# Split weights kept in DRAM by the first band of a hybrid streaming encoder; weights in pieces of four row tiles

## The chip, the cores and the metric

The kernel runs on one core of one Trainium2 chip. The metric is the device time of one execution in microseconds (us). Every time below is from that chip.

## What is computed

One layer of a hybrid encoder, on 2048 frames of a new stream and 32 frames of a running one (2080 columns in all, width 1024). Cut to what matters:

```
hn  = rmsnorm(x, norm1);   proj = hn @ w_in            # 1024 x 3072
ya  = RG-LRU group, yb = RWKV-7 group, yc = mLSTM group   # of proj, causal
x   = x + concat(ya, yb, yc) @ w_out                   # 1024 x 1024
gu  = rmsnorm(x, norm2) @ w_ffn_in                     # 1024 x 5632
x   = x + (silu(gu[..., :2816]) * gu[..., 2816:]) @ w_ffn_out   # 2816 x 1024
out = rmsnorm(x, norm_f), and the mixers' new states
```

All of it is float32.

## The kernel before, in words

Activations lie with the features on the 128 partitions and frames along the columns. The frames are cut into four **bands**: 512, 512, 512 and 544 (two blocks of 272). For each band there is an input normalisation (`innorm`), an input projection (`inproj`, 24 output tiles of 128 features), the three mixers on groups of 128 frames (`mixers`, `group`), and a second half (`phase2`: the output projection of 8 tiles, 44 tiles of the first FFN matrix in six groups, and after each group the 8 output tiles of the second FFN matrix over the 4 or 3 row tiles of that group). The program records `inproj` of all four bands first, then by turns `mixers(i)` and `phase2` of band i.

**Products.** Every big product is made with float32r operands in two parts. A value x is written as hi (its float32r copy, by ScalarE) plus lo (x - hi, by VectorE): `split`, line 618. `mm3` (623) then issues three matmuls for each row tile of 128 and each block of columns: hi x hi, hi x lo, lo x hi, summed in PSUM. The weights are read from DRAM again in every band, and split again.

**Weights.** `load_w` (590) fetches one weight tile of kt row tiles (8, or 4 and 3 for the second FFN matrix). It takes a slot for the parts, a pair `wh`, `wl` of 128 x 1024 of which there are WB = 2 (a tile of 4 or fewer row tiles takes half of one), loads the raw float32 data into one of RB = 2 buffers `raw` of 128 x 1024, and splits it. In the input projection every second tile goes, in two halves of four row tiles, into the tiles `hh0` to `hh3` and `hl0` to `hl3`, which `phase2` uses for the split FFN activations. The last group of the last band puts four of its weight tiles into activation tiles that are no longer needed (`into`).

**Order of the work.** Nothing is issued as it is written. A `Recorder` (148) takes down every instruction with a level, and `order` (244) plans them on five queues (TensorE, VectorE, ScalarE, GpSimd, and SP, which issues nearly all DMAs). Each takes, of what is ready in the plan, the lowest level first. The levels are a pair, the second for TensorE: `EVAC` (-2), `WGT` (-1; loads and splits of weights), `NORM` (0), `MIX` (1; the mixers), `PROJ` (0, and 2 on TensorE) and `LATE` (2). So on TensorE the mixers' matmuls go before those of the projections, in bursts that `order` holds back by a debt (RATE, BURST, GATHER, WAIT). Durations come from `cost` (348). A DMA costs its bytes at 360 per ns, one after the other:

```python
            if best == "dma":
                free[best] = when + 475.0
                dma_end = max(dma_end, free[best] + 650.0) + o.dur
                o.end = dma_end
                free[best] = max(free[best], dma_end - WINDOW)
```

The resulting order of each queue is fixed. On the chip each engine works through it and waits for semaphores where something is late. So an instruction that waits holds up all that stands behind it on its queue. All instructions have line 332 (`emit`) in the profile; they are told apart by the names of their tiles: `pj` is the PSUM tile of the projections, `rw` and `ml` those of the mixers, `ah`/`al` and `hh`/`hl` split activations.

**The mixers' round trip.** In `rwkv`, for each group of 128 frames, a small matrix goes from `Hr` to DRAM (`tb<-Hr`, four DMAs), comes back repeated on 96 partitions (`xs<-tb`, one DMA of 384 KB, here called the broadcast), is worked on by 62 short VectorE instructions in a row (`utmp`, `Z`), goes to DRAM once more (`zb<-Z`) and back (`c<-zb`). There are 17 groups.

Of the kernel before, what the change touches and what calls it, by code (L numbers as in the profile page):

```python
# [11 lines left out]
F32 = mybir.dt.float32  # L12
F32R = mybir.dt.float32r
# [12 lines left out]
NFF = 22  # L26
# [95 lines left out]
PSLACK = 300.0  # L122
XB = 8
ACCB = 2
WB = 2
RB = 2
HG = 4
SQB = 3
# [293 lines left out]
def hybrid_kernel(ctx, tc, A, O, cfg):  # L422
# [161 lines left out]
                return y[:, a:b, col - c0:col - c0 + n]  # L584


    half = [None]
    wide = [0]

    def load_w(src, kt, eng=None, many=False, into=None):  # L590


        if many:
            wide[0] += 1
        if into is not None:
            parts = [tuple(t[:, :kt * 128] for t in into)]
        elif many and wide[0] % 2:
            f = wide[0] // 2 % 2 * 2
            parts = [tuple(hp.tile([128, HW], F32R, tag=f"{x}{f + h}", name="w" + x)[:, :512] for x in ("hh", "hl"))
                     for h in range(2)]  # L600
        elif kt <= 4 and half[0] is not None:
            parts = [tuple(t[:, 512:512 + kt * 128] for t in half[0])]
            half[0] = None
        else:
            slot = tuple(wp.tile([128, 1024], F32R, tag=x, name=x) for x in ("wh", "wl"))
            half[0] = slot if kt <= 4 else None
            parts = [tuple(t[:, :kt * 128] for t in slot)]
        level, rec.level = rec.level, WGT
        raw = wp.tile([128, 1024], F32, tag="raw", name="raw", bufs=RB)[:, :kt * 128]
        kp = kt // len(parts)  # L610
        for h, (wh, wl) in enumerate(parts):
            r = raw[:, h * kp * 128:(h + 1) * kp * 128]
            SY.dma_start(r.rearrange("p (k m) -> p k m", k=kp), src[:, h * kp:(h + 1) * kp, :])
            split(wh, wl, r, eng)
        rec.level = level
        return [tuple(t[:, k * 128:k * 128 + 128] for t in pt) for pt in parts for k in range(kp)]

    def split(hi, lo, x, eng=None):

        S.activation(hi, x, AF.Copy)  # L620
        (eng or V).tensor_tensor(out=lo, in0=x, in1=hi.bitcast(F32), op=ALU.subtract)
# [72 lines left out]
    def innorm(i):  # L694
# [20 lines left out]
        if i == 0:  # L715
            level, rec.level = rec.level, WGT
            load(0)
            SY.dma_start(vec, A["vecs"])
            for m, ks in enumerate(((1, 2), (3, 4), (5, 6, 7))):
                first_w.append(load_w(w_in(m), 8, V, True))  # L720
                for k in ks:
                    load(k)
            rec.level = level
            setup()
            for k in range(8):
                act.append(act_tiles(k, n))
                split_x(*act[k], x[k], VV("norm1", k))
                if k > 1:
                    square(k - 2)
            square(6)  # L730
            square(7)
        else:
            for k in range(8):
                level, rec.level = rec.level, LATE
                load(k)
                rec.level = level
                square(k)
# [7 lines left out]
    def inproj(i):  # L745
# [32 lines left out]
        for m in range(24):  # L778
            if m == NEXT and i + 1 < len(cfg.sb1):
                innorm(i + 1)  # L780
            w = first_w.pop(0) if first_w else load_w(w_in(m), 8, V, True)
            pss = proj(w, act, [x_[:2] for x_ in segs])
            for (o, N, sg), ps in zip(segs, pss):
                if late is not None:
# [591 lines left out]
    def phase2(c0, blks, HG, last=False):  # L1376
# [27 lines left out]
                V.tensor_tensor(out=acc[:, o:o + N], in0=acc[:, o:o + N], in1=sq, op=ALU.add)  # L1404

        for d in range(8):
            w = load_w(A["w_out"][d], 8)
            for (o, N), ps in zip(bl, proj(w, act, bl)):
                rec.level = EVAC
                V.tensor_tensor(out=x2[d][:, o:o + N], in0=x2[d][:, o:o + N], in1=ps, op=ALU.add)  # L1410
                rec.level = NORM
            accum(d, 0, n)
# [13 lines left out]
        for kg in groups:  # L1426
            hs = []
            for f in range(f0, f0 + kg):
                wg = load_w(A["w_ffn_in"][f], 8)
                wu = load_w(A["w_ffn_in"][NFF + f], 8)  # L1430
                hh = hp.tile([128, HW], F32R, tag=f"hh{f - f0}", name=f"hh{f - f0}")[:, :n]
                hl = hp.tile([128, HW], F32R, tag=f"hl{f - f0}", name=f"hl{f - f0}")[:, :n]
                us = []
                for (o, N), pg in zip(bl, proj(wg, act, bl)):
                    rec.level = EVAC
# [15 lines left out]
            for bs in ([[b] for b in bl] if end and last else [bl]):  # L1451
                for d in range(8):
                    if d not in ws:
                        ws[d] = load_w(A["w_ffn_out"][d][:, f0:f0 + kg, :], kg, into=act[d] if end and last and d > 3 else None)
                    for (o, N), ps in zip(bs, proj(ws[d], hs, bs)):
                        rec.level = EVAC
                        V.tensor_tensor(out=x2[d][:, o:o + N], in0=x2[d][:, o:o + N], in1=ps, op=ALU.add)
                        rec.level = NORM
                        if end:
                            accum(d, o, N)  # L1460
                            S.activation(x2[d][:, o:o + N], x2[d][:, o:o + N], AF.Copy, scale=VV("norm_f", d))
# [15 lines left out]
    mls = Pool("mls", 1)  # L1477
    dt_ = Pool("dt", 2, space=DRAM)
    ap_ = Pool("act", 1)
    wp = Pool("wp", WB)  # L1480
    ev = Pool("ev", 2)
    hp = Pool("hp", 1)
    UN = [rws.tile([128, 3, 2, 64], F32, name=f"Un{c}") for c in range(2)]
    for u in UN:
        G.memset(u, 0.0)
# [152 lines left out]
```

## Time and profile before

| | |
|---|---|
| median of 3 runs | 2850.44 us (2846.54 to 2855.05) |
| the profiled execution's own time | 2846.7 us |
| its span, first to last instruction | 2844.9 us |
| TensorE, VectorE, ScalarE busy | 2749.6, 2146.1, 1281.1 us |
| mean granted TensorE clock | 0.987 |
| DMA | 317.92 MB, mean 112 GB/s |
| HBM read, written | 268.50 MB, 46.27 MB |

All views below are of that one execution. Busy is the time in which an engine worked on at least one instruction; matmuls overlap, and the end of each is modelled, so TensorE's busy time tells above all where it was idle. The granted clock is the share of its full speed that TensorE was allowed. A wait is put down to what came last by the profile.

### The profile page before, as it was taken

Reading aid. Unit: us, or ns where it says so; the run is one execution under the profiler, and the core shown is the slowest. Engines: PE = TensorE matmul, PEld = TensorE weight load, DVE = VectorE, ACT = ScalarE, POOL = GpSimd, SP = SyncE. Lnnn points to the kernel's source line nnn. Section 1 sums busy time; section 2 is a strip of 40 time slices with the busy share of each in tenths; the row PEclk is TensorE's granted clock in tenths of the full one; section 3 lists DMA queues with packets and bytes.
Section 4 is the critical chain, followed back from the end, with each engine's and each line's share of the span. In section 5 each row is a group of like instructions: output and inputs, shape, how many; then the busy total and the mean of one; then the engine's idle time right before and its main releaser. Section 6 shows DMA issues by size and latency. Waiting matters only on the chain. (4 is left out here: it accounts for less than half of the span.)

```text
span 2844.9 us, 48298 instructions
## 1 busy us (share of the span) xinstructions
PE 2749.6 (97%) x17609; PEld 2310.6 (81%) x17609; DVE 2146.1 (75%) x6009; ACT 1281.1 (45%) x2830; POOL 43.7 (2%) x170
## 2 busy tenths in 40 slices
PE   9999999999999999999999999999999999999998
PEld 7877777889777777777777777777787778999997
DVE  6778877877887878789878888888676676554555
ACT  5555554655553444455444444454433334322223
POOL 0000000000000000000000000000000000000000
PEclk9999999999999999999999999999999999999999
DMA  7453534444323333335233333353332235232232
GB/s 238 133 168 116 179 105 143 138 132 121 121 72 108 88 100 99 95 112 160 73 108 98 89 96 94 100 162 78 100 109 83 84 89 161 81 89 87 88 93 77
DMA packets 235210, 317.92 MB, mean 112 GB/s; under 512 B 63100, under 2 KB 146988, under 8 KB 234844
## 3 DMA queue, kind: packets, MB, share of 16 engines
q1 hardware_dynamic: 233820, 313.72, 37.3%
q8 instruction: 138, 2.26, 0.3%
q10 hardware_dynamic: 1152, 1.11, 0.1%
q14 instruction: 100, 0.82, 0.1%
HBM read 268.50 MB, written 46.27 MB: 111 GB/s over the span
## 5 line engine op out<-in xcount | busy, mean ns | idle before, releaser
L332 PE MATMUL pj<-ah,wh 128*128 128x512 f32 (+1 forms) x2560 | 898.7, 359 | 3.2 <-ACT wh L332 1.1
L332 PE MATMUL pj<-al,wh 128*128 128x512 f32 (+1 forms) x2560 | 898.9, 358 | 2.5 <-DVE al L332 2.5
L332 PE MATMUL pj<-ah,wl 128*128 128x512 f32 (+1 forms) x2560 | 828.8, 356 | 1.5 <-DVE wl L332 1.5
L332 ACT ACTIVATE wh<-raw 128x1024 fp32r<-128x1024 f32 (+2 forms) x444 | 382.3, 861 | 728.8 <-PE pj L332 604.8
L332 PEld LDWEIGHTS pj<-ah,wh 128*128 128x128 f32 x2560 | 484.5, 190 | 68.7 <-ACT ah L332 1.6
L332 PEld LDWEIGHTS pj<-al,wh 128*128 128x128 f32 x2560 | 486.7, 190 | 63.9 <-DVE al L332 3.4
L332 PEld LDWEIGHTS pj<-ah,wl 128*128 128x128 f32 x2560 | 454.9, 189 | 66.8 <-DVE wl L332 3.1
L332 DVE TENSOR_TENSOR wl<-raw,wh 128x1024 fp32r<-128x1024 f32 (+2 forms) x444 | 433.0, 976 | 62.1 <-ACT wh L332 56.4
L332 PE MATMUL pj<-hh,wh 128*128 128x512 f32 (+1 forms) x856 | 299.6, 360 | 9.4 <-ACT hh L332 9.2
L332 PE MATMUL pj<-hl,wh 128*128 128x512 f32 (+1 forms) x856 | 300.9, 359 | 0.1
L332 PE MATMUL pj<-hh,wl 128*128 128x512 f32 (+1 forms) x856 | 280.9, 357 | 0.0
L332 DVE TENSOR_TENSOR x<-x,pj 128x512 f32<-128x512 f32 (+1 forms) x280 | 159.2, 584 | 126.4 <-PE pj L332 122.3
L332 PEld LDWEIGHTS pj<-hh,wh 128*128 128x128 f32 x856 | 160.9, 189 | 35.1 <-ACT hh L332 13.8
L332 PEld LDWEIGHTS pj<-hl,wh 128*128 128x128 f32 x856 | 162.3, 190 | 22.6 <-DVE hl L332 1.7
L332 PE MATMUL pj<-ah,hh 128*128 128x512 f32 (+1 forms) x480 | 170.1, 361 | 6.6 <-ACT hh L332 5.8
L332 PEld LDWEIGHTS pj<-hh,wl 128*128 128x128 f32 x856 | 152.8, 189 | 22.2
L332 PE MATMUL pj<-al,hh 128*128 128x512 f32 (+1 forms) x480 | 169.6, 360 | 0.0
L332 PE MATMUL pj<-ah,hl 128*128 128x512 f32 (+1 forms) x480 | 156.9, 359 | 0.0
L332 DVE TENSOR_TENSOR utmp<-Z,xs 96x60 f32<-96x60 f32 (+27 forms) x527 | 107.0, 203 | 59.1 <-DMA xs<-tb 52.5
L332 DVE TENSOR_TENSOR stg<-stg,pj 128x512 f32<-128x512 f32 (+1 forms) x110 | 62.5, 584 | 91.9 <-PE pj L332 91.3
L332 DVE TENSOR_TENSOR cbuf<-pj,acc 128x512 f32<-128x512 f32 (+1 forms) x110 | 62.7, 586 | 68.9 <-PE pj L332 66.8
L332 DVE TENSOR_TENSOR Z<-Z,utmp 96x60 f32<-96x60 f32 (+27 forms) x527 | 106.6, 202 | 6.4
(344 smaller groups left out, 3835.2 us busy)
## 6 DMA issues: line engine op xcount, KB each, us to landing
raw<-in_w_ffn_in SPq DMA_DIRECT2D x176, 512.0 KB, 3.6
raw<-in_w_ffn_out SPq DMA_DIRECT2D x128, 256.0 KB, 2.7
raw<-in_w_in SPq DMA_DIRECT2D x96, 256.0 KB, 3.1
raw<-in_w_in SPq DMA_DIRECT2D x48, 512.0 KB, 4.1
spill<-stg SPq DMA_DIRECT2D x72, 256.0 KB, 2.9
raw<-in_w_out SPq DMA_DIRECT2D x32, 512.0 KB, 3.5
x<-in_xT SPq DMA_DIRECT2D x48, 256.0 KB, 5.4
raw<-in_w_ffn_out SPq DMA_DIRECT2D x64, 192.0 KB, 2.4
```

Of the source, the lines that this page charges most:

```text
L332: o.fn(*o.args, **o.kw)
```

## The change

`load_w` gets a key for each weight tile and works in pieces of four row tiles (or fewer). The first time that a piece is asked for, it is loaded and split as before, and then both parts are written to a DRAM scratch tensor of its own (`kept`), at level `NORM`. Each later time both parts are loaded from there, in one DMA where they lie in one tile, and nothing is split. The slots are now WB = 5 tiles of 128 x 2 x 512 that hold both parts of a piece, and the raw buffers two of 128 x 512. The eight tiles `hh`, `hl` become one tile `HT`. The calls of `load_w` only get their key.

```diff
--- before.py
+++ after.py
@@ -122,7 +122,7 @@
 PSLACK = 300.0
 XB = 8
 ACCB = 2
-WB = 2
+WB = 5
 RB = 2
 HG = 4
 SQB = 3
@@ -584,36 +584,42 @@
                 return y[:, a:b, col - c0:col - c0 + n]
 
 
-    half = [None]
     wide = [0]
-
-    def load_w(src, kt, eng=None, many=False, into=None):
-
-
-        if many:
-            wide[0] += 1
-        if into is not None:
-            parts = [tuple(t[:, :kt * 128] for t in into)]
-        elif many and wide[0] % 2:
-            f = wide[0] // 2 % 2 * 2
-            parts = [tuple(hp.tile([128, HW], F32R, tag=f"{x}{f + h}", name="w" + x)[:, :512] for x in ("hh", "hl"))
-                     for h in range(2)]
-        elif kt <= 4 and half[0] is not None:
-            parts = [tuple(t[:, 512:512 + kt * 128] for t in half[0])]
-            half[0] = None
-        else:
-            slot = tuple(wp.tile([128, 1024], F32R, tag=x, name=x) for x in ("wh", "wl"))
-            half[0] = slot if kt <= 4 else None
-            parts = [tuple(t[:, :kt * 128] for t in slot)]
+    kept = {}
+
+    def load_w(key, src, kt, eng=None, many=False, into=None):
+
+
+
+        wide[0] += many
         level, rec.level = rec.level, WGT
-        raw = wp.tile([128, 1024], F32, tag="raw", name="raw", bufs=RB)[:, :kt * 128]
-        kp = kt // len(parts)
-        for h, (wh, wl) in enumerate(parts):
-            r = raw[:, h * kp * 128:(h + 1) * kp * 128]
-            SY.dma_start(r.rearrange("p (k m) -> p k m", k=kp), src[:, h * kp:(h + 1) * kp, :])
-            split(wh, wl, r, eng)
+        out = []
+        for h in range(0, kt, 4):
+            kp = min(4, kt - h)
+            m = kp * 128
+            if into is not None:
+                parts = [(into[x][:, :m], x) for x in range(2)]
+            elif many and wide[0] % 2:
+                f = wide[0] // 2 % 2 * 4 + h // 2
+                parts = [(HT[:, f:f + 2, :m], slice(0, 2))]
+            else:
+                parts = [(wp.tile([128, 2, 512], F32R, tag="w", name="w", bufs=WB)[:, :, :m], slice(0, 2))]
+            hl = into if into is not None else [parts[0][0][:, x, :] for x in range(2)]
+            rec.level = WGT
+            if (key, h) in kept:
+                for t, x in parts:
+                    SY.dma_start(t.bitcast(F32), kept[key, h][:, x, :])
+            else:
+                kept[key, h] = dp.tile([128, 2, m], F32, name="kept" + "_".join(map(str, key)) + f"_{h}")
+                raw = wp.tile([128, 512], F32, tag="raw", name="raw", bufs=RB)[:, :m]
+                SY.dma_start(raw.rearrange("p (k m) -> p k m", k=kp), src[:, h:h + kp, :])
+                split(hl[0], hl[1], raw, eng)
+                rec.level = NORM
+                for t, x in parts:
+                    SY.dma_start(kept[key, h][:, x, :], t.bitcast(F32))
+            out += [tuple(t[:, k * 128:k * 128 + 128] for t in hl) for k in range(kp)]
         rec.level = level
-        return [tuple(t[:, k * 128:k * 128 + 128] for t in pt) for pt in parts for k in range(kp)]
+        return out
 
     def split(hi, lo, x, eng=None):
 
@@ -717,7 +723,7 @@
             load(0)
             SY.dma_start(vec, A["vecs"])
             for m, ks in enumerate(((1, 2), (3, 4), (5, 6, 7))):
-                first_w.append(load_w(w_in(m), 8, V, True))
+                first_w.append(load_w(("in", m), w_in(m), 8, V, True))
                 for k in ks:
                     load(k)
             rec.level = level
@@ -778,7 +784,7 @@
         for m in range(24):
             if m == NEXT and i + 1 < len(cfg.sb1):
                 innorm(i + 1)
-            w = first_w.pop(0) if first_w else load_w(w_in(m), 8, V, True)
+            w = first_w.pop(0) if first_w else load_w(("in", m), w_in(m), 8, V, True)
             pss = proj(w, act, [x_[:2] for x_ in segs])
             for (o, N, sg), ps in zip(segs, pss):
                 if late is not None:
@@ -1404,7 +1410,7 @@
                 V.tensor_tensor(out=acc[:, o:o + N], in0=acc[:, o:o + N], in1=sq, op=ALU.add)
 
         for d in range(8):
-            w = load_w(A["w_out"][d], 8)
+            w = load_w(("out", d), A["w_out"][d], 8)
             for (o, N), ps in zip(bl, proj(w, act, bl)):
                 rec.level = EVAC
                 V.tensor_tensor(out=x2[d][:, o:o + N], in0=x2[d][:, o:o + N], in1=ps, op=ALU.add)
@@ -1426,10 +1432,9 @@
         for kg in groups:
             hs = []
             for f in range(f0, f0 + kg):
-                wg = load_w(A["w_ffn_in"][f], 8)
-                wu = load_w(A["w_ffn_in"][NFF + f], 8)
-                hh = hp.tile([128, HW], F32R, tag=f"hh{f - f0}", name=f"hh{f - f0}")[:, :n]
-                hl = hp.tile([128, HW], F32R, tag=f"hl{f - f0}", name=f"hl{f - f0}")[:, :n]
+                wg = load_w(("fi", f), A["w_ffn_in"][f], 8)
+                wu = load_w(("fi", NFF + f), A["w_ffn_in"][NFF + f], 8)
+                hh, hl = [HT[:, 2 * (f - f0) + x, :n] for x in range(2)]
                 us = []
                 for (o, N), pg in zip(bl, proj(wg, act, bl)):
                     rec.level = EVAC
@@ -1451,7 +1456,7 @@
             for bs in ([[b] for b in bl] if end and last else [bl]):
                 for d in range(8):
                     if d not in ws:
-                        ws[d] = load_w(A["w_ffn_out"][d][:, f0:f0 + kg, :], kg, into=act[d] if end and last and d > 3 else None)
+                        ws[d] = load_w(("fo", d, f0), A["w_ffn_out"][d][:, f0:f0 + kg, :], kg, into=act[d] if end and last and d > 3 else None)
                     for (o, N), ps in zip(bs, proj(ws[d], hs, bs)):
                         rec.level = EVAC
                         V.tensor_tensor(out=x2[d][:, o:o + N], in0=x2[d][:, o:o + N], in1=ps, op=ALU.add)
@@ -1477,9 +1482,10 @@
     mls = Pool("mls", 1)
     dt_ = Pool("dt", 2, space=DRAM)
     ap_ = Pool("act", 1)
-    wp = Pool("wp", WB)
+    wp = Pool("wp", 1)
     ev = Pool("ev", 2)
     hp = Pool("hp", 1)
+    HT = hp.tile([128, 2 * HG, HW], F32R, name="HT")
     UN = [rws.tile([128, 3, 2, 64], F32, name=f"Un{c}") for c in range(2)]
     for u in UN:
         G.memset(u, 0.0)
```

## Rows read from the trace of the kernel before

**Rows 1.** The page, busy time of each engine with its share of the span

```profile
PE 2749.6 (97%) x17609; PEld 2310.6 (81%) x17609; DVE 2146.1 (75%) x6009; ACT 1281.1 (45%) x2830; POOL 43.7 (2%) x170
```

**Rows 2.** Stretches: us, busy per engine (xcount), granted clock, DMA share, GB/s

```profile
0.00:60.00 60.00, 53.40 (x231) 42.60 (x232) 41.68 (x103) 32.07 (x65) 4.32 (x26) 1.00 0.75 255
60.00:135.00 75.00, 74.71 (x358) 60.71 (x357) 57.02 (x109) 42.08 (x91) 0.50 (x2) 1.00 0.43 135
135.00:730.00 595.00, 570.00 (x3965) 487.93 (x3964) 468.39 (x1474) 329.28 (x859) 10.10 (x38) 0.98 0.46 137
730.00:1326.00 596.00, 584.26 (x3554) 463.22 (x3552) 501.94 (x1474) 275.31 (x601) 10.47 (x40) 0.99 0.36 107
1326.00:1900.00 574.00, 554.20 (x3366) 440.29 (x3367) 478.98 (x1410) 264.45 (x578) 10.19 (x38) 0.99 0.36 104
1900.00:2400.00 500.00, 483.18 (x2731) 387.58 (x2731) 363.62 (x941) 203.55 (x407) 8.11 (x26) 0.98 0.34 99
...
2485.00:2769.00 284.00, 284.00 (x2264) 284.00 (x2263) 140.70 (x286) 75.31 (x125) 0.00 (x0) 1.00 0.31 89
2769.00:2845.00 76.00, 61.97 (x485) 60.79 (x483) 45.41 (x120) 28.98 (x60) 0.00 (x0) 0.92 0.26 79
```

**Rows 3.** The chain of waits from 1660 us: start us, us, what

```profile
1660.47 3.02 PE pj L332 x13
...
1671.30 2.89 DMA tb<-Hr
...
1674.27 6.83 DMA xs<-tb
```

**Rows 4.** TensorE's waits: us in total, times, longest us

```profile
PE pj L332 <- ACT hh L332: 15.0, 7, 5.8
...
PE pj L332 <- DVE wl L332: 1.5, 3, 0.5
...
PE pj L332 <- ACT wh L332: 1.1, 1, 1.1
```

**Rows 5.** The waits of all engines, VectorE for the broadcast

```profile
DVE utmp L332 <- DMA xs<-tb: 52.5, 17, 6.3
```

**Rows 6.** Busy time by stretch as in rows 2, behind one broadcast

```profile
1684.60:1687.60 3.00, 0.06 (x1) 0.00 (x0) 2.92 (x12) 0.63 (x1) 0.00 (x0) 0.85 0.39 94
1687.60:1694.00 6.40, 6.37 (x24) 4.71 (x24) 3.38 (x12) 1.98 (x6) 0.00 (x0) 0.54 0.15 44
```

**Rows 7.** The sum over 13 stretches of 14 us behind broadcasts

```profile
sum 182.00, PE 155.76 PEld 126.33 DVE 159.28 ACT 65.49 POOL 0.23; mean PE 11.98 PEld 9.72 DVE 12.25 ACT 5.04 POOL 0.02
```

**Rows 8.** Weight splits, page and by shape: xcount | busy, mean | idle before

```profile
L332 ACT ACTIVATE wh<-raw 128x1024 fp32r<-128x1024 f32 (+2 forms) x444 | 382.3, 861 | 728.8 <-PE pj L332 604.8
...
L332 DVE TENSOR_TENSOR wl<-raw,wh 128x1024 fp32r<-128x1024 f32 (+2 forms) x444 | 433.0, 976 | 62.1 <-ACT wh L332 56.4
...
L332 DVE TENSOR_TENSOR wl<-raw,wh 128x1024 fp32r<-128x1024 f32 x256 | 312.3, 1220 | 30.7 <-ACT wh L332 25.8 <-DMA c<-zb 2.0 <-ACT ta L332 0.8
...
L332 DVE TENSOR_TENSOR hl<-raw,hh 128x512 fp32r<-128x512 f32 x96 | 65.6, 686 | 18.5 <-ACT hh L332 17.5 <-PE pj L332 0.3
...
L332 ACT ACTIVATE hh<-raw 128x512 fp32r<-128x512 f32 x96 | 59.9, 627 | 55.9 <-PE pj L332 54.4 <-DMA raw<-in_w_in 0.8
```

**Rows 9.** DMA to 60 and 135 us: GB/s by slice, issues, landing us

```profile
GB/s 0 192 232 283 296 381 400 407 394 446 399 406 378 339 335 373 408 389 388 167 0 0 238 356 105 15 335 134 341 322 240 115 77 0 76 314 305 88 276 263
...
raw<-in_w_in SPq DMA_DIRECT2D x6, 512.0 KB, 4.5
...
raw<-in_w_in SPq DMA_DIRECT2D x26, 256.0 KB, 3.7
```

**Rows 10.** DMA issues from 730 to 1326 us

```profile
raw<-in_w_ffn_in SPq DMA_DIRECT2D x45, 512.0 KB, 3.5
```

**Rows 11.** Timeline, SP and VectorE near 440 us: start, length [idle before]

```profile
436.41 0.65 SPq L332 DMA_DIRECT2D xs<-tb  x1
...
444.69 0.19 DVE L332 TENSOR_TENSOR utmp<-Z,xs 96x31 f32<-96x31 f32 x1 [4.18 <-DMA xs<-tb]
```

## The prediction

> **What bounds the kernel now.** First the busy line of the page [rows 1]: TensorE is busy 97% of a span of 2844.9 us, VectorE 75%, ScalarE 45%. So the reader goes on to where TensorE is not busy, by stages [rows 2]. The loads of each weight show the stages: `w_in` of the first band until about 135 us, the other three input projections until 730, the second half of bands 0, 1 and 2 until 1326, 1900 and 2400, that of band 3 to the end. Between 2485 and 2769 us TensorE is busy for 284.00 of 284 us: 2264 matmuls, 125 ns each, no gap. With 512 columns the chain has 13 in 3.02 us, 232 ns [rows 3]. The idle time is 2844.9 - 2749.6 = 95.3 us: 6.9 before 135 us, 25.0 to 730, then 11.7, 19.8 and 16.8 in the three mixed stages (73.3 from 135 to 2400), and 14 at the very end. The granted clock adds to that: 0.98 to 0.99 from 135 us on and 0.92 at the end, worth (1 - clock) x stretch, some 40 us.
>
> What are these gaps? Not weights: TensorE waited 1.1 us for a `wh` and 1.5 us for a `wl` in the whole run [rows 4]. The longest total, 15.0 us, is for `hh`, the split of an activation. One place comes back in every group of 128 tokens: the broadcast `xs<-tb`, on which VectorE sits 52.5 us in 17 waits [rows 5]. In the chain it takes 6.83 us [rows 3]. What stands behind it on VectorE is late, and TensorE's next instruction with it: 2.9 us idle of the 3.0 from 1684.6, then a clock of 0.54 (close to the lower level, 1.2 of 2.4 GHz) until 1694 [rows 6]. In 13 windows of 14 us behind the 13 longest of these waits TensorE is idle for 182 - 155.76 = 26.2 us [rows 7]. So TensorE is the bound, its loss is made of late landings and of what queues behind them, and the weight path is hidden.
>
> **The change, part by part.** A weight piece is four row tiles: 256 KB raw, 512 KB as two parts. A band has 48 + 16 + 88 + 48 = 200 of them, 51.4 MB raw.
>
> *Splits removed.* Three of four bands lose theirs. VectorE loses 0.75 x (433.0 + 65.6) = 374 us, ScalarE 0.75 x (382.3 + 59.9) = 332 us [rows 8]. In the first band 64 splits of 1024 columns become two of 512: 64 x (2 x 0.686 - 1.220) = +10 us of VectorE. Net VectorE goes from 2146 to about 1780 us. None of this stands on TensorE's path directly (1.1 + 1.5 us). It helps indirectly, as fewer instructions stand behind a late landing. Splits are some 20% of VectorE's time; I take 20% of the 44 us of idle that is neither at the start (6.9), at the end (14) nor behind the broadcast (30, the 26.2 and what lies before those windows), 9 us, and one split of 0.69 us behind each of 17 broadcasts at the 0.6 that TensorE loses of such a wait (below), 7 us. Term: -16 us (bounds: 0, and half of the 73.3 us of idle and half the clock loss of these stages, -37 - 17 = -54).
>
> *Writes in the first band.* Its input projection adds 24 x 1 MB = 25.2 MB to a stage that already moves 188 GB/s on average (255 and 135 in its two stretches [rows 2]). In the first 60 us 15.3 MB move and 24 pieces would be written: (15.3 + 12.6) MB / 60 us = 465 GB/s, while the plateau of the slices from 9 to 18 us is about 400 (highest 446) [rows 9]. Moved at 400, these bytes need 70 us: up to +10, less what can be put off (the next band's x, loaded at lowest level; two raw buffers of 512 columns fetch less ahead than two of 1024). Second, each raw buffer is half as big. Its cycle is landing + 0.63 + 0.69 + some 0.1 us; at 3.7 us [rows 9] two buffers give a piece every 2.6 us, at 4.5 us every 2.95, and TensorE uses one in 12 x 0.232 = 2.78. The second costs 0.17 x 48 = 8 us. Bounds 0 and 18; I take +8, as the stage is between these rows. The Trainium skill (HBM Reference, Specifications) gives a core an effective 358 GB/s; the slices here pass 400, so the trace disagrees while this core runs alone. By 358 the 27.9 MB would need 78 us, and the bound would be +18 from the bytes alone.
>
> *The first band's second half* adds 77.6 MB of writes in 596 us, +130 GB/s on 107: by that stage's own ratio (0.36 of the engines at 107) the DMA share goes to 0.80. A piece is needed every 596/152 = 3.9 us, so two raw buffers suffice up to a landing of 6.4 us. A slot comes free when its write has landed, 5 to 6 us after the split by the landing of 512 KB (3.5 [rows 10]) with a queue ahead, while TensorE works on the four slots before it for 11 us: no cost. What is behind the write on SP's queue waits for VectorE's `lo`, as the next raw load did before.
>
> *Loads of both parts* in bands 1 to 3: +12.6 MB an input projection (+64 GB/s, share 0.46 to about 0.66) and +38.8 MB a second half (+68, 0.36 to 0.59). The load now waits for TensorE's release of a slot; before, the raw load waited for VectorE, which waited for ScalarE, which waited for the same release, so nothing on SP's queue (the mixers' `tb`, `zb` and `xs` among it) stands longer than before. Four other pieces cover a landing: 11 us against 3.5 to 5. In the pure stretch at the end it is 512 KB per 3.0 us, 175 GB/s: no cost, and no gain, as TensorE has no gap there. SP issues about 460 more DMAs; it mostly waits: nothing.
>
> *What is late next:* the mixers' round trips share the rings with twice the weight bytes. The broadcast took 6.83 us at a share of 0.36 [rows 3] and 8.3 us (436.41 to 444.69 [rows 11]) in the stage of 0.46. A group takes 2265/17 = 133 us from 135 to 2400. I take +2.2 us for the 596/133 = 4.5 groups at 0.80 and +1 us for the other 12.5: 22 us of VectorE; TensorE loses about 0.6 of such a wait today (30 of 52.5), +13, and two more spells at the lower clock, +5. Term: +18 (bounds 0 and +60, the second rival's price).
>
> *Without cost:* one tile `HT` in place of eight, five half slots in place of four (the same bytes of SBUF), the last projection's loads into the activations' tiles (no split behind them, two DMAs each in place of one).
>
> **Sum:** 2846.7 (the profiled execution: span and 1.8 us around it) - 16 + 8 + 18 = 2856.7. The profiled execution is 3.7 us under the median of 2850.4, so the forecast is 0.2% over the median: no change that a measurement of this kernel can tell (0.3%, 8.5 us). Its own range is 2842 to 2875.
>
> **Rivals.** *A, the relief wins.* With VectorE down from 84% to some 65% busy in the mixed stages a late landing leaves no queue behind it. Between 40% and half of the idle time and of the lower clock from 135 to 2400 us goes: -(29 to 37) - (13 to 17), first band +8, landings unchanged: 2801 to 2813; I say 2810, as the smaller share asks less of it. For it: where VectorE is busy 84% of a stage, a late landing mostly has work behind it. Against it: the idle share is highest (25.0 of 595) where VectorE is less busy (79%) and DMA busier (0.46), and lower (11.7 of 596) where VectorE is at 84% and DMA at 0.36: idle follows the DMA.
>
> *B, landings stretch, slower.* The place is the round trip of every group, Hr to `tb` in DRAM and back: two landings, 17 times. If each takes 1.5 us more (what the broadcast took more at 0.46 than at 0.36), and TensorE waits for all of it, 17 x 2 x 1.5 = 51, clock +9, first band +8, relief -10: 2846.7 + 58 = 2905. It decides once a landing is later by more than TensorE's queue now absorbs, (52.5 - 30) / 17 = 1.3 us. For it: [rows 5, 11]. Against it: 52.5 us of waits cost TensorE only some 30. The Trainium skill (DMA: Bandwidth & Descriptors, Latency and other measured facts) has HBM access at 0.2 us on average and 2 us under high load, which speaks against this change; 1.8 us twice in 17 groups would be 61 us, about 2915. The trace bears out only part of that: 512 KB land in 4.5 us at a share of 0.75 and in 3.5 at 0.36 [rows 9, 10].
>
> *C, the first band starves.* If raw landings there get as long as the broadcast's 6.8 us [rows 3], two buffers give a piece every 4.1 us: (4.1 - 2.78) x 24 pieces before mixers can fill in, (4.1 - 3.9) x 152 after: +32 + 30, 2906. Against it: prefetched pieces and mixers' work cover short delays.
>
> **How the numbers follow.** Forecast 0.42 (0.25 of it within 0.3% of the median, 0.14 above, 0.03 below), A 0.30, B 0.18, C 0.10. Faster 0.33, same 0.25, slower 0.42. Range 2805 to 2905: it takes in most of A and reaches to B and C; some 0.08 lies below and 0.10 above. Both signs are likely, so the forecast's own range stands above.
>
> **What would show it.** Right: 200 weight splits on each of ScalarE and VectorE, none over 512 columns; VectorE near 1780 us; DMA near 575 MB (318, 103 more written, 154 more read); DMA share near 0.8 from 730 to 1326 us; the wait for `xs<-tb` up from 52.5 to 65 to 80 us; idle from 135 to 2400 us near 75 to 85 us; TensorE still without a gap in the last stretch. Wrong: the wait for `xs<-tb` or the idle time clearly down (A); TensorE waiting for `w` in the first band (C); idle up by over 40 us with lower clock behind it (B).

## The result and the profile after

The changed kernel took 2892.7 us (median of 4 runs, 2892.05 to 2898.84), the one before 2850.23 beside it: a ratio of 1.0153 [1.0132, 1.0173], so 1.5% slower. That lies inside the range of the prediction (2805 to 2905), but above the forecast of 2857 and above its own range (2842 to 2875). The profiled execution took 2892.28 us, with a span of 2890.4; 45.5 us more than the span of before.

First the page of the changed kernel: its busy line, the line of DMA, and the two groups of weight splits that are left there (24 more are written `HT<-raw`, 15.1 us on ScalarE and 16.5 on VectorE).

```profile
PE 2761.1 (96%) x17609; PEld 2316.0 (80%) x17609; DVE 1831.4 (63%) x5665; ACT 982.9 (34%) x2486; POOL 43.7 (2%) x170
...
DMA packets 321416, 574.84 MB, mean 199 GB/s; under 512 B 70460, under 2 KB 164588, under 8 KB 321052
...
L332 ACT ACTIVATE w<-raw 128x512 fp32r<-128x512 f32 (+1 forms) x176 | 108.6, 618 | 146.5 <-PE pj L332 107.8
...
L332 DVE TENSOR_TENSOR w<-raw,w 128x512 fp32r<-128x512 f32 (+1 forms) x176 | 118.2, 673 | 19.8 <-ACT w L332 18.4
```

Against [rows 1] the change did what it says: VectorE lost 315 us, ScalarE 298, and 200 splits of weights are left on each. TensorE has the same 17609 matmuls. Its span grew by 45.5 us in two parts: idle from 95.3 to 2890.4 - 2761.1 = 129.3 us (+34.0), and busy time from 2749.6 to 2761.1 (+11.5) for the same work. The second part goes with the clock: 0.982 on average in place of 0.987, which by (1 - clock) x span is 52 us in place of 37, 15 more where 11.5 were measured.

Where the idle time lies is read from the stretches of [rows 2], here of the changed kernel (us, busy per engine with its count, granted clock, DMA share, GB/s):

```profile
0.00:60.00 60.00, 52.20 (x229) 41.58 (x230) 38.13 (x102) 29.30 (x62) 4.30 (x26) 1.00 0.98 346
60.00:135.00 75.00, 70.05 (x306) 55.03 (x306) 55.72 (x109) 40.97 (x90) 0.50 (x2) 0.98 0.91 319
135.00:730.00 595.00, 561.69 (x3880) 468.69 (x3881) 424.15 (x1511) 263.62 (x770) 10.62 (x42) 0.98 0.64 203
730.00:1326.00 596.00, 570.08 (x3654) 459.44 (x3652) 486.45 (x1527) 275.12 (x665) 10.46 (x40) 0.98 0.68 222
1326.00:1900.00 574.00, 552.01 (x3317) 439.47 (x3316) 393.08 (x1278) 186.48 (x479) 11.98 (x41) 0.98 0.58 173
1900.00:2400.00 500.00, 486.93 (x2582) 387.88 (x2582) 259.42 (x692) 115.08 (x262) 5.84 (x19) 0.99 0.60 183
2400.00:2485.00 85.00, 75.17 (x531) 72.12 (x530) 38.57 (x84) 23.99 (x39) 0.00 (x0) 0.94 0.64 206
2485.00:2769.00 284.00, 284.00 (x2261) 283.84 (x2260) 85.22 (x220) 24.20 (x62) 0.00 (x0) 1.00 0.57 175
```

Stretch less TensorE's busy time, before and after: 6.9 and 12.7 us up to 135; 25.0 and 33.3 to 730; 11.7 and 25.9 to 1326; 19.8 and 22.0 to 1900; 16.8 and 13.1 to 2400; 15.0 and 22.2 in the rest. The greatest loss, 14.2 us, stands in the first band's second half, the stage that writes the kept weights; there VectorE is still busy 82% of the time (84% before), since the splits stay. The stretches are fixed in time, while the changed kernel comes to its stages later (the first store of `out_yT` for the first band is issued at 1295 us before and at 1373 after). With the bounds moved along, to 153, 793, 1404, 1977 and 2448 us, its idle time is 13.0, 34.8, 25.2, 24.7, 18.0 and 13.6 us: the loss in the first band's second half stands (13.5 us), another 9.8 us lie in the three later input projections, and the lower value from 1900 to 2400 us doesn't stand, though VectorE's load fell furthest there (from 73% to 52%).

What the engines wait for, in the changed kernel (us in total, times, longest):

```profile
PE pj L332 <- ACT HT L332: 22.2, 7, 6.4
PE rw L332 <- DVE ta L332: 13.8, 6, 4.9
PE ml L332 <- DVE wide L332: 13.0, 5, 4.0
PE pj L332 <- DVE x L332: 8.7, 1, 8.7
...
DVE utmp L332 <- DMA xs<-tb: 83.3, 17, 7.5
```

`HT` is now the tile of the split activations as well; the wait for it answers to `hh` in [rows 4]. No load of a weight stands here. In the kernel before, the waits for `ta` and `wide` were short:

```profile
PE rw L332 <- DVE ta L332: 3.8, 4, 1.6
...
PE ml L332 <- DVE wide L332: 2.2, 2, 1.7
```

`ta` is made from what the second round trip brings back (`c`). `wide` is a tile of the mLSTM mixer that needs nothing from the broadcast: the order put its instructions on VectorE between the first `utmp` and the next, so they stand when the broadcast is late. Two of the five waits for `wide`, 7.7 of the 13.0 us, have the broadcast in their chain (near 436 and 1673 us). VectorE's wait for the broadcast went from 52.5 us [rows 5] to 83.3. The chain of waits of the changed kernel (start, us, what) shows the group of [rows 3]:

```profile
1660.65 4.08 DMA tb<-Hr
...
1664.74 8.54 DMA xs<-tb
...
1673.30 0.19 DVE utmp L332
1673.49 0.08 DVE wide L332
```

Both landings got longer: 4.08 us for 2.89, 8.54 for 6.83, together 2.9 us in this group. Over all 17 groups the first `utmp` starts 8.3 us after SP issues the broadcast, 7.1 before; VectorE waits for it each time in both. In the waits from 730 to 1326 us, the changed kernel has

```profile
PE pj L332 <- ACT HT L332: 5.0, 1, 5.0
PE rw L332 <- DVE ta L332: 4.9, 1, 4.9
...
DVE utmp L332 <- DMA xs<-tb: 14.8, 4, 6.1
DVE ta L332 <- DMA c<-zb: 8.1, 4, 4.2
```

and the kernel before, in the last two,

```profile
DVE utmp L332 <- DMA xs<-tb: 8.5, 4, 4.4
...
DVE ta L332 <- DMA c<-zb: 1.3, 2, 0.9
```

These two waits grew by 13.1 us, TensorE's idle time in the stage by 14.2.

One gap is new, and in no part of the prediction. From 2425.87 TensorE stands 8.7 us for the last band's x. The chain has

```profile
2398.26 27.62 PE pj L332 x168
...
2427.49 6.44 DMA x<-in_xT
...
2434.05 0.45 DVE x L332
2434.50 0.04 issue
2434.55 10.52 PE pj L332 x61
```

and SP's own timeline shows why x is issued so late: ahead of it in that queue are loads of kept weights that wait for TensorE to release a slot (`w<-keptout`, six of which take SP 13.97 us from 2406.22) and stores of `out_yT`. Before, TensorE's waits have no such line.

### The profile page after: what moved, and what is told of

Its sections match the earlier page's. It is cut to its first block, busy times and chain, and to the rows that moved or that the text cites. A ratio compares the mean times of both kernels' runs of the same rounds, so it can differ in the third digit from the quotient of the medians.

```text
span 2890.4 us, 47945 instructions
## 1 busy us (share of the span) xinstructions
PE 2761.1 (96%) x17609; PEld 2316.0 (80%) x17609; DVE 1831.4 (63%) x5665; ACT 982.9 (34%) x2486; POOL 43.7 (2%) x170
## 2 busy tenths in 40 slices
DMA packets 321416, 574.84 MB, mean 199 GB/s; under 512 B 70460, under 2 KB 164588, under 8 KB 321052
## 4 chain that ended last, share of the span: by engine, by line
PE 63%; DVE 17%; DMA 14%; ACT 3%; issue 2%; SPq 1%; DVEq 0%; ACTq 0%
PE pj L332 52%; PE rw L332 7%; DMA xs<-tb 4%; PE ml L332 3%; DVE x L332 2%; DMA raw<-in_w_in 2%; DVE stg L332 1%; DVE w L332 1%; DMA tb<-Hr 1%; DVE utmp L332 1%; DVE Z L332 1%; DMA zb<-Z 1%; DMA x<-in_xT 1%; DMA c<-zb 1%; SPq L332 1%
## 5 line engine op out<-in xcount | busy, mean ns | idle before, releaser
L332 PE MATMUL pj<-ah,w 128*128 128x512 f32 (+1 forms) x5120 | 1409.3, 358 | 11.4 <-DVE x L332 8.7
L332 PEld LDWEIGHTS pj<-ah,w 128*128 128x128 f32 x5120 | 901.3, 190 | 140.4 <-DVE x L332 8.9
L332 PE MATMUL pj<-al,w 128*128 128x512 f32 (+1 forms) x2560 | 898.4, 358 | 0.0
L332 PE MATMUL pj<-HT,w 128*128 128x512 f32 (+1 forms) x2568 | 526.1, 360 | 16.5 <-ACT HT L332 15.5
L332 PEld LDWEIGHTS pj<-al,w 128*128 128x128 f32 x2560 | 487.3, 190 | 61.9 <-DVE al L332 0.4
L332 PEld LDWEIGHTS pj<-HT,w 128*128 128x128 f32 x2568 | 420.5, 190 | 87.5 <-ACT HT L332 18.6
L332 PE MATMUL pj<-ah,HT 128*128 128x512 f32 (+1 forms) x960 | 277.5, 365 | 7.6 <-ACT HT L332 6.7
L332 PEld LDWEIGHTS pj<-ah,HT 128*128 128x128 f32 x960 | 172.3, 192 | 35.1 <-ACT HT L332 7.6
L332 PE MATMUL pj<-al,HT 128*128 128x512 f32 (+1 forms) x480 | 171.3, 363 | 0.5 <-DVE al L332 0.5
L332 DVE TENSOR_TENSOR utmp<-Z,xs 96x60 f32<-96x60 f32 (+27 forms) x527 | 107.3, 204 | 90.8 <-DMA xs<-tb 83.3
L332 DVE TENSOR_TENSOR w<-raw,w 128x512 fp32r<-128x512 f32 (+1 forms) x176 | 118.2, 673 | 19.8 <-ACT w L332 18.4
```

What stands on the lines that cost most here:

```text
L332: o.fn(*o.args, **o.kw)
```

## The experiments

The question was which of four things cost the time: the pieces of four row tiles (costed at nothing), the writes, the loads of both parts, or, common to all, a fixed order that was planned with landings too short. The planner counts 475 + 650 ns for the issue of a DMA, its bytes at 360 per ns and 950 ns until it can be used: 3.2 us for the 384 KB of the broadcast, where the chains have 6.83 and 8.54. Each group of runs was timed beside the kernel before, whose median differs a little from group to group.

**One part at a time.** Four kernels take the changed code and put back or leave out parts (the edits are cut to what matters). e3_loads and e4_relief compute with the weights of eight pieces, so they show times and no results.

```diff
 # e1_pieces: every band loads raw and splits; nothing is kept
-            if (key, h) in kept: ... else: ...
+            raw = wp.tile([128, 512], F32, tag="raw", name="raw", bufs=RB)[:, :m]
+            SY.dma_start(raw.rearrange("p (k m) -> p k m", k=kp), src[:, h:h + kp, :])
+            split(hl[0][:, :m], hl[1][:, :m], raw, eng)
 # e2_writes: as e1_pieces, and the first band's writes, which nobody reads
+            if (key, h) not in kept:
+                kept[key, h] = dp.tile([128, 2, m], F32, name=...)
+                rec.level = NORM
+                for t, x in parts:
+                    SY.dma_start(kept[key, h][:, x, :], t.bitcast(F32))
 # e3_loads: eight pieces alone are kept; later bands load both parts of one of these
-                    SY.dma_start(t.bitcast(F32), kept[key, h][:, x, :])
+                    SY.dma_start(t.bitcast(F32), few[kept[key, h] % 8][:, x, :m])
 # e4_relief: as e3_loads, but one part is loaded: the bytes of a raw piece, and no split
+                SY.dma_start(hl[0][:, :m].bitcast(F32), few[kept[key, h] % 8][:, 0, :m])
```

> The pieces alone: weights in pieces of four row tiles, five slots, half as big raw buffers, the tile HT, but every band loads the raw weights and splits them; nothing is written by or read back. Traffic theory (the loss comes from later landings beside the added bytes): no added bytes, so 2840 to 2860 us, wait for the broadcast xs<-tb near 52 us. Pieces theory (smaller raw buffers, more and shorter splits, another plan): most of the loss is here already, 2875 to 2893 us.

> Pieces plus the writes of the first band, but nobody reads them: the later bands load raw weights and split. Traffic theory: the writes fill the queues until 1326 us only, 2860 to 2875 us, TensorE's idle time up by 10 to 20 us before 1326 us and not after. First-band theory (starved raw buffers, the whole loss is there): 2885 to 2895 us. Pieces theory: the same as the pieces alone.

> The loads of both parts in bands 1 to 3 without the writes: the first band keeps only 8 of its 200 pieces, and the later bands load these 8 in turn (so the later bands compute with wrong weights; bytes, shapes and instructions are those of the changed kernel). Traffic theory: the loads cost 10 to 25 us, the relief of VectorE gives back up to 15: 2855 to 2875 us, wait for the broadcast 65 to 80 us. First-band theory: no loss, 2835 to 2850 us.

> The relief alone: the later bands split nothing and load only one part, 256 KB a piece as before the change, from the same 8 kept pieces (the low part is left as it was, so the results are wrong). Bytes are those of the kernel before, VectorE and ScalarE have the work of the changed kernel. Traffic theory: 2825 to 2845 us, as fewer instructions stand behind late landings. If the relief is worth nothing, 2845 to 2855 us; if the removed splits make the waits worse (less filling work ahead of the broadcast), over 2860 us.

Measured, beside 2846.25 us for the kernel before: e1_pieces 2865.44, 1.0072 [1.0048, 1.0096]; e2_writes 2895.53, 1.0170 [1.0140, 1.0199]; e3_loads 2873.89, 1.0098 [1.0072, 1.0124]; e4_relief 2844.86, 0.9999 [0.9985, 1.0014]. As differences: pieces +19, the splits of three bands away -20.6 (e4 against e1), 154 MB more to load +29 (e3 against e4), 103 MB more to write +30 (e2 against e1) or +16 on top of the loads (1.0153 - 1.0098 of 2846). 19 - 21 + 29 + 16 gives 43, the change, by construction: the 16 are what is left. With the +30 the sum would be 57, so the parts don't simply add up.

The expectations were met in part. e3_loads and e4_relief came where the traffic theory had them (e4 at its upper end). e1_pieces took more than that theory allowed and less than the pieces theory, and e2_writes took more than any theory had, by the time nearest to the first band's; the traces tell why it wasn't that.

Two things in the traces bear on it. First the wait for the broadcast, in the order e1, e2, e3, e4 (VectorE's waits, one line of each kernel):

```profile
DVE utmp L332 <- DMA xs<-tb: 61.6, 17, 5.6
...
DVE utmp L332 <- DMA xs<-tb: 52.6, 15, 5.4
...
DVE utmp L332 <- DMA xs<-tb: 78.8, 17, 10.3
...
DVE utmp L332 <- DMA xs<-tb: 61.6, 17, 7.5
```

The loads lengthen it (78.8 against 61.6 with the same work on the engines), the relief alone doesn't shorten it. From SP's issue to the first `utmp` it is 8.2 us in e3 and 7.0 in e4. Second, where the writes cost. The stretches of e1_pieces, then of e2_writes:

```profile
0.00:135.00 135.00, 126.00 (x583) 102.12 (x584) 101.60 (x224) 73.49 (x160) 4.86 (x28) 1.00 0.56 184
...
730.00:1326.00 596.00, 579.18 (x3505) 463.99 (x3504) 500.85 (x1537) 283.98 (x649) 10.38 (x40) 0.99 0.35 103
```

```profile
0.00:135.00 135.00, 123.60 (x534) 96.16 (x534) 93.88 (x210) 70.45 (x152) 4.87 (x28) 0.99 0.94 331
...
730.00:1326.00 596.00, 564.87 (x3417) 449.58 (x3416) 480.38 (x1454) 278.23 (x636) 10.38 (x40) 0.98 0.68 224
```

TensorE's idle time goes from 9.0 to 11.4 us in the first stage, though the engines of the DMA are full there, and from 16.8 to 31.1 in the second half, at a share of 0.68. The writes cost where mixers run beside them, not where raw weights are short. The pair with and without the change agrees (11.7 and 25.9). In the second half VectorE's wait for the broadcast grows from 10.5 to 14.6 us and that for `c<-zb` from 0.4 to 3.1, together about half of the 14.3 us; what the other half waits for is spread over many small waits and stays open. Over the whole run e2's wait for the broadcast is no longer than e1's (52.6 and 61.6): the writes lengthen it in their own stage only. The spans of the two profiled executions differ by 20 us (2865.0 and 2885.2), half of it idle time (111.9 and 121.5) and half TensorE's busy time (2753.1 and 2763.7), at mean clocks that hardly differ (0.982 and 0.983), so that this half isn't explained; the medians differ by 30, so this +30 is the least certain of the terms.

**What the plan believes.** One line of the planner's `cost` tells it 4 us more for the broadcast alone; nothing that is computed changes, only the order.

```diff
-        return b / 360.0, 950.0
+        return b / 360.0, 950.0 + (4000.0 if ins[0].ap[0][0] == 0 and n == 1024 else 0.0)
```

As a control of what any other order is worth, `SLACK`, the planner's allowance for work on the mixers' way, goes from 40 to 50 ns in both kernels.

> The kernel before; only the planner is told that the broadcast xs<-tb lands 4 us later than it thought (it took 7.1 us on average, planned 3.2). Same instructions, other order. Theory that TensorE's loss is the gap between plan and landing: VectorE gets other work ahead of the first use, the 52 us of waits fall under 25 us, idle time falls by 15 to 35 us, 2810 to 2835 us. If the order is a lottery in which one late landing is as good as another: 2835 to 2865 us.

> The changed kernel with the same 4 us told to the planner. Landing theory: the 83 us of waits for the broadcast fall by half, 2850 to 2875 us. If the loss sits elsewhere (weights, first band), 2880 to 2900 us.

> The kernel before with the planner's SLACK at 50 ns in place of 40: nothing is added or removed, only the order of the queues changes. It measures what any new order is worth. If orders differ little, 2840 to 2856 us and the 20 us of the pieces alone are the pieces' own; if orders are a lottery, over 10 us to either side.

> The changed kernel with SLACK at 50 ns: the same question there. If the loss is the added traffic, 2880 to 2905 us; if the changed kernel only drew a bad order, it could be anywhere from 2850 us on.

Measured, beside 2849.42: f1_before_plan 2837.66, 0.9952 [0.9935, 0.9969]; f2_after_plan 2828.88, 0.9924 [0.9905, 0.9944]; p1_before_slack 2864.61, 1.0053 [1.0036, 1.0071]; p2_after_slack 2888.71, 1.0125 [1.0093, 1.0156].

The same line is worth 0.5% to the kernel before and 2.3% to the changed one, so that the changed kernel is now faster than both originals. f2_after_plan moves the same 574.84 MB at a share no lower than before the line, yet VectorE's wait for the broadcast falls from 83.3 us to

```profile
DVE utmp L332 <- DMA xs<-tb: 14.7, 10, 3.3
```

and the stretches that lost most are these:

```profile
135.00:730.00 595.00, 575.21 (x4053) 486.18 (x4052) 422.46 (x1486) 268.50 (x781) 10.55 (x42) 0.99 0.66 209
730.00:1326.00 596.00, 574.28 (x3487) 459.22 (x3486) 492.52 (x1495) 281.83 (x653) 10.10 (x38) 0.99 0.70 233
1326.00:1900.00 574.00, 565.35 (x3542) 450.02 (x3541) 417.62 (x1383) 198.14 (x512) 12.40 (x43) 1.00 0.61 182
```

Idle time there is 19.8, 21.7 and 8.6 us, against 33.3, 25.9 and 22.0 in the changed kernel, and TensorE's busy time falls from 2761.1 to 2734.5 as the clock rises from 0.982 to 0.991 ((1 - clock) x span: 25 us in place of 52). The bytes are as many and as crowded, and the broadcast doesn't land sooner: in the ten groups where VectorE still waits, the first `utmp` starts 8.0 us after the issue of the broadcast (8.3 in the changed kernel). What went is VectorE's wait.

In the kernel before, the landing theory failed. f1_before_plan took 2837.66 us, where the lottery had it and the theory 2810 to 2835, and its wait for the broadcast all but went,

```profile
DVE utmp L332 <- DMA xs<-tb: 9.4, 5, 4.6
```

while TensorE's idle time, which was to fall by 15 to 35 us, rose from 95.3 to 100.0: 36.2 us of it lie from 1900 to 2400 us, 16.8 before. f2_after_plan took less than either theory had. So a wait of VectorE is not by itself a loss of TensorE. p1_before_slack came out as the lottery had it (15 us to one side), p2_after_slack as the traffic theory had it.

The control puts a bound on the reading: a mere other order moves a kernel by +0.5% (before) or -0.3% (changed). The 2.3% lie well outside that; the 0.5% that the line brings to the kernel before, and the 0.7% of the pieces, do not.

**Relief, pieces and order under the corrected plan.** The 4 us are told to e4_relief and e1_pieces, and, with a `SLACK` of 50, to both originals.

> The relief alone (bytes of the kernel before, no splits in bands 1 to 3) with the planner's 4 us for the broadcast. Against the changed kernel with the same 4 us (0.992 of before) it is the price of the added bytes under that plan: if the bytes cost only by landing later than planned, they are now nearly free, 2815 to 2830 us; if they cost by themselves (starved weights, fuller queues), 2795 to 2812 us. It leaves the low part of the later bands' weights as it was.

> The pieces alone with the planner's 4 us. If the pieces' 0.7% was the waits for the broadcast and the order drawn, it comes out with the kernel before and the 4 us, 2830 to 2845 us; if smaller raw buffers and shorter splits cost of themselves, 2850 to 2865 us.

> The kernel before, 4 us told, SLACK 50 ns: a second order for the same work. If the 4 us are worth 0.5 to 1% in any order, 2830 to 2850 us (SLACK 50 without them took 2864.6); if the first order was lucky, over 2855 us.

> The changed kernel, 4 us told, SLACK 50 ns. If telling the planner is what turns the change from a loss into a gain, 2820 to 2840 us and below the kernel before with the same two settings; if the first order was lucky, 2850 us and over.

Measured, beside 2849.88: g1_relief_plan 2782.24, 0.9764 [0.9746, 0.9782]; g2_pieces_plan 2861.2, 1.0042 [1.0028, 1.0055]; g3_before_plan_slack 2853.25, 1.0009 [0.9997, 1.0021]; g4_after_plan_slack 2829.03, 0.9932 [0.9910, 0.9954].

With the plan corrected, the splits of three bands are worth 2861.2 - 2782.2 = 79 us in place of 21, and the bytes still cost 2828.9 - 2782.2 = 47 us, as they did under the old price. In ratios, to be free of the rounds: the bytes are worth 1.54% without the line (1.0153 against 0.9999) and 1.60% with it (0.9924 against 0.9764), 44 and 46 us. And the line brings 2.35% to the kernel that has the relief and not the bytes (e4 to g1), 2.3% to the one that has both, 0.5% and 0.3% to the two that split in every band (before to f1, e1 to g2). So the line doesn't make the bytes cheaper: the added 4 us pay where the splits are gone, with or without the bytes. Of the 79 us some 37 are idle time from 1900 to 2400 us (46.4 us in g2, 9.0 in g1), about which more below.

g1_relief_plan took less than both of its theories had and is nearer to the one by which the bytes cost by themselves; g2_pieces_plan came where the pieces were to cost of themselves, g3_before_plan_slack between its two theories, g4_after_plan_slack where the plan was to turn the loss into a gain.

g1_relief_plan, which leaves the low part of the weights unloaded, shows what the relief alone reaches: TensorE 98% busy, at a clock of 0.996.

```profile
PE 2720.2 (98%) x17609; PEld 2295.8 (83%) x17609; DVE 1828.7 (66%) x5665; ACT 985.8 (35%) x2486; POOL 43.7 (2%) x170
...
DVE utmp L332 <- DMA xs<-tb: 6.2, 5, 2.6
```

Two orders of the changed kernel agree (2828.9 and 2829.0), two of the kernel before don't (2837.7 and 2853.3). In g2_pieces_plan and g3_before_plan_slack one stage, 1900 to 2400 us, is idle for 46.4 and 42.2 us, where the two originals have 16.8 and 13.1. The traces show what stands there. From 2300 to 2400 us TensorE waits, in g2,

```profile
PE rw L332 <- DVE ta L332: 22.7, 1, 22.7
PE pj L332 <- ACT ah L332: 7.2, 1, 7.2
PE rw L332 <- DVE yx L332: 5.3, 1, 5.3
```

and the same three in g3 (22.6, 7.2, 5.3) and in f1 (16.8, 7.2, 5.3). It is the second round trip of the last group of frames, which comes when no projection of the third band is left beside it to keep TensorE busy: in g3 the group's broadcast is issued at 2333.62 us, in the kernel before at 2299.10, and there projections fill TensorE until 2365. p1_before_slack has the last two of these waits and 6.8 us of the first; its stage is idle for 36.5 us. Every kernel that doesn't split in the later bands has 9 to 15 us in this stage, those that split 14 to 46. From f1 to f2 the idle time falls by 21.7 us in this stage and grows by 11.8 in all the others together: the changed kernel's lead under the corrected plan comes from this one place. Why the orders with splits leave it uncovered stays open. So does the pieces' own cost: +19 and +24 us in the two pairs (e1 against before, g2 against f1), with a control that moves by 15.

The version to keep is the changed kernel with the line of f2_after_plan: 2828.9 us, 0.8% under the kernel before, and 2.2% under the change as it was made.

## Why the prediction was right or wrong

The likeliest outcome, no measurable change, was not what came; the side it called likeliest (slower, 0.42) and the reason were. The sum of the terms was +10 us and the measured change +42: the time lies in the range because that reached to rivals B and C, not because the sum came out. It lies between the forecast and rival B, and by B's mechanism: *landings stretch*.

- *Splits removed*, -16: measured -20.6 (e4 against e1). The size is right for this plan, though a mere other order moves as much as 15 us; under the corrected plan the same splits were worth 79. But VectorE's busy line was put at 1780 us, and it is 1831. The groups of splits did lose 364 us as worked out (498.6 to 134.7). The step that failed is to take a group's sum off the busy line: the means of rows hold time in which neighbours on the engine overlap. All of VectorE's groups add up to 2417 us before and 2051 after, 366 less, while the busy line fell by 315.
- *Writes in the first band*, +8 in its input projection and nothing in its second half: measured +16 to +30, the place wrong. The first 135 us cost 5.8 us of idle time; the plateau of 400 GB/s didn't hold with writes in it (below). The larger part, some 14 us in the pair before and after and in e1 against e2, is the second half, where "no cost" looked at raw buffers, slots and SP's queue, and left out that the mixers' round trips run there as well. They were priced one paragraph on, under *what is late next*, at 2.2 us for 4.5 groups; VectorE's waits for `xs<-tb` and `c<-zb` grew by 13.1 us there. The round trip through `zb` was in no term. The DMA share in the stage came to 0.68, not 0.80.
- *Loads of both parts*, and with them *what is late next*, +18: measured +29 for the loads alone. The wait for `xs<-tb` was to be 65 to 80 us; it is 83.3. Idle time from 135 to 2400 us was to be 75 to 85; it is 94.3. Mechanism right, size over a third too small. Part of what was missed is the queue: the loads of kept weights wait on SP for a slot, and x of the last band stood behind them. "Nothing on SP's queue stands longer than before" was wrong there, by 8.7 us.
- *Without cost*, the pieces and slots: measured +19, which a re-ordering of the same work can bring as well (+15). Open.
- Rival A, *the relief wins*: refuted for the change as it stands, where the relief brings 21 us and the bytes cost twice that. What A left out is the plan: with it corrected and no bytes added (g1_relief_plan) 67 us go, 30 more than in A's own sum. A's argument against itself, "idle follows the DMA", held for the change as it stands and not in general: f2_after_plan moves the same bytes and is idle for 90.1 us, the kernel before for 95.3.
- Rival B: the landings got longer by 1.2 and 1.7 us in the group shown; B had 1.5 each. Its 51 us assumed that TensorE waits for all of it; idle time from 135 to 2400 us grew by 21 us. The page it named, the Trainium skill's DMA: Bandwidth & Descriptors (Latency and other measured facts), has 0.2 us of HBM latency on average and 2 under high load, 1.8 more. The landings here stretched by less, 1.2 and 1.7 us at a share of 0.6; what part of that is the latency of HBM no run shows.
- Rival C, *the first band starves*: refuted. No wait for a raw weight is among TensorE's but the very first of the run, with the DMA at 0.98 and 0.91. (Its sum, 2846.7 + 32 + 30, is 2909, not 2906.)
- The last stretch was to have no gap: 284.00 of 284 us, right. 575 MB: 574.84.

What no part of the prediction saw is how much the order decides. The added bytes cost about the same under both prices of the broadcast (44 and 46 us), but the removed splits were worth 21 us under one and 79 under the other. It asked what is late next; the chain with `wide` shows how a late landing can hold up work that doesn't need it, where the plan has put that work right behind the moment at which it believed the landing done. How much of the time goes that way the runs don't show: in f1_before_plan and g2_pieces_plan nearly all of VectorE's wait for the broadcast went (9.4 and 1.4 us are left), and TensorE was idle no less than before (100.0 and 116.2 us, after 95.3 and 111.9 without the line).

## What to carry to other kernels

Where the order of the work is fixed ahead by a planner, compare its price of each transfer with the landing in the trace, and correct that first: the same change was 1.5% slower under the wrong price of one transfer and not slower under the corrected one (0.9924 [0.9905, 0.9944] against 0.9952 [0.9935, 0.9969], and in a second order 0.9932 against 1.0009). What the correction freed here was the worth of the work taken away, while the added bytes cost the same; only runs with each part alone, under both prices, could tell. Time an order that differs for no reason as a control, and don't explain differences below what it moves. When work is taken off an engine and put on DMA, price every round trip that shares the rings in that stage, the ones of the stages that only write too. And look for the last link of a serial chain: where the order leaves no other work beside it, TensorE stands for all of it.

## What was not expected of the hardware

With raw loads and writes of split weights together the DMA engines were full from 20 to 60 us, and moved less than the prediction's plateau. The stretches of the changed kernel:

```profile
20.00:40.00 20.00, 19.71 (x105) 16.59 (x104) 14.77 (x50) 10.35 (x25) 0.00 (x0) 1.00 1.00 357
40.00:60.00 20.00, 19.68 (x86) 15.52 (x85) 8.44 (x13) 7.54 (x17) 0.00 (x0) 1.00 1.03 359
```

At a share of 1.00 and 1.03 that is 357 and 359 GB/s. The prediction read 400 from single slices of 1.5 us [rows 9], which single slices after the change reach too (up to 436). In the first 60 us 20.8 MB moved (346 GB/s) where 27.9 were asked for, and still TensorE's idle time there grew by 1.2 us only (53.40 us busy before, 52.20 after); the 75 us behind them lose 4.7 more. So the first band's input projection puts off some of the traffic, and not all of it for nothing. The Trainium skill (HBM Reference, Specifications) gives a core an effective 358 GB/s as its half of a domain with two cores, and about 425 to a core that streams alone. The prediction used the first figure alone and called it contradicted. Here one core ran, and over 40 us of full engines, with reads and writes mixed, this trace comes to the first figure and not to the second; whether it is the writes that make the difference no run shows.

The other is the clock. Both kernels do the same matmuls, and TensorE's busy time was 2749.6, 2761.1, 2734.5 and 2720.2 us in the kernels before, after, f2_after_plan and g1_relief_plan, at mean clocks of 0.987, 0.982, 0.991 and 0.996. In these four it goes with the idle time (95.3, 129.3, 90.1 and 60.0 us): behind a gap the clock is lower for some us [rows 6], so that such a gap is paid for more than once. From g1_relief_plan to the changed kernel idle time is 69 us longer and busy time 41. Not all of the busy time follows the clock: f1_before_plan has the clock of the kernel before (0.987), 4.7 us more idle time and 15.0 us less busy time (2734.6), and why stays open.
